# A hybrid attention and S5 layer: GpSimd's tables in parts of three instructions, the chunk operator in its own frame, parameters behind a longer wait

## The chip, the core and the metric

One core of one Trainium2 chip. The time is the device time of one execution in microseconds; three executions were timed, and one more was profiled. PE is TensorE, PEld its weight loads, DVE VectorE, ACT ScalarE, POOL GpSimd, SP SyncE (here only a DMA queue); ACTq is the DMA issue on ACT's queue.

## The reference, cut to what matters

```python
h = rms_norm(x, norm_gain)                       # (2048, 1024)
q, k, v, z_attn, u_ssm, z_ssm, g = split(h @ w_in)
attn = windowed_gqa(q, k, v, sink, rel_table) * silu(z_attn)
# S5: 32 groups of 16 channels, 64 complex states, two directions
a_bar = exp(lam * dt); b_bar = b * (a_bar - 1) / lam
xs = associative_scan(x_t = a_bar * x_{t-1} + b_bar u_t)     # forwards and backwards
y = d * u + sum over directions of Re(c x)
ssm = glu(gelu(y)) * silu(z_ssm)
merged = sigmoid(g_attn) * (attn @ wa) + sigmoid(g_ssm) * (ssm @ ws)
out = rms_norm(x + merged @ w_out) * final_norm_gain
```

All in float32 of (1, 2048, 1024). The matrix products are made of three float32r products each: a value is split into a high part (a copy to float32r) and a low part (the value less its high part).

## The kernel before, in words

**Order of work.** The program is one hand-written order of instructions; each engine takes its own in that order. The projections run as a main line: a weight of 128 output columns is loaded by SP, its high part `wh` is copied by ACT (L163), its low part `wl` subtracted by POOL in four instructions (L155), and 24 matmuls a token block (`mm3`, L220 to L222, three for each of eight slices) add up into one of three PSUM banks "pj", which ACT or DVE empties (`evac`). `wnext` splits a weight one ahead of the one in use. Side chains are generators. At fixed places of the main line (`turn`: after every sixth matmul of a projection) each side gets half its rate as credit and runs a step, up to its next `yield`, while credit is above zero.

**Stage 1** makes h of block b+1 (`make_h`, a side with RATE1) beside six projections of block b. At block 2 `ssm_params` starts: it issues its DMAs from SP's queue (a, dt, b, c, eye, d), then, from the next projection on as a side with rate RATEP, transposes of a, dt and c on PE (L478, L486), and some 300 short instructions on DVE (L441), six a step. After block 3 `drain(pr)` runs what is left.

**Stage 2** is the other projections for blocks 2 and 3 (rate RATE2), three gate weights for all blocks with h of blocks 0 and 1 read back (`h_split`), then blocks 0 and 1. Beside it runs `chain`: first `ssm`, later attention, later the preparation of the last stage. The last stage (GLU, branches, output) has no part in the change.

**The scan** (`ssm`) goes through 8 chunks of four groups, one `frame` each, 19 steps a frame. A position is one of T = 8 in a piece; a piece is one of M = 256. For a chunk:
- `prep_w` (POOL, 12 instructions of 128x256 in `product`, L692 to L694): the table `wt`; `mats` transposes it on PE (L775, banks "s2") and splits it into Wh, Wl (L778, L769).
- `prep_e` (POOL, 6 instructions for each half of a chunk): tables `ec`, `es` of the phases; `mirror_e` copies their mirrored half (ACT, L724).
- `prep_o` (DVE, 6 instructions of 128x512): the table `wo`; `split_o` splits it into ws.
- `zmat`: the chunk operator. `sign_o` (ACT, L739, L741) negates half of `wo`; matmuls with `wo` (L800) and with c (L807) fill two "s2" banks; copies (L808, L809) and one instruction (L810) on DVE make Z of 128x240, stored to DRAM (L904); `load_m` (four DMAs from ACT's queue) reads it back shifted, and `split_m` splits it into Mh, Ml.
- `inject` (PE L837, ACT L838, L839) makes X; `rotate` (DVE L846 to L849), `scan` (DVE L858), `rotate` back, for each half; `high_h` (ACT L865) and `low_h` (DVE L870) split the result into Hh, Hl; `emit` (PE L880 with M and U, L884 with ws and H, ACT L888) makes y, two steps a half.

Before, `frame(i)` for chunk i had, by step: 1 inject 0 and 2 inject 1 with the end of zmat(i); 3 rotate of half 0, store of Z, inject 2; 4 scan, inject 3; 5 rotate back, load_m, mats(i+1); 6 prep_e(i+1, 0), mats; 7 prep_w(i+2), split_o; 8 split_m, high_h; 9 low_h, rotate of half 1; 10 scan; 11 rotate back, prep_e(i+1, 1); 12 and 13 emit half 0; 14 high_h; 15 low_h, mirror_e(i+1, 0); 16 prep_o(i+1), split_u; 17 and 18 emit half 1, split_u, mirror_e(i+1, 1), load_u(i+2) and sign_o(i+1); 19 the L800 matmuls of zmat(i+1).

Banks: "pj" 3, "s1" 2, "s2" 2. wt, wo, ws, Z, M and H have one buffer each, ec and es two.

Of the kernel before, what the change touches and what calls it, by code (L numbers as in the profile page):

```python
# [7 lines left out]
F32 = mybir.dt.float32  # L8
# [3 lines left out]
AF = mybir.ActivationFunctionType  # L12
# [12 lines left out]
M = S // T  # L25
GB = 4
RATE1 = 1.336
RATEP = 2.2
RATE2 = 1.237
RATE3 = 1.499  # L30
WLAG = 2
# [6 lines left out]
def kernel(  # L38
# [404 lines left out]
    def ssm_params(pool):  # L443
# [224 lines left out]
    def ssm(pool):  # L668
# [7 lines left out]
        def bc(t, i, wide):  # L676
            return t[:, i * GB:(i + 1) * GB].unsqueeze(3 if wide else 2).to_broadcast(sh)

        def product(o, p, q, eng):

            for n, (a, b, c, d, op) in enumerate(
                ((p[0], q[0], p[1], q[1], ALU.subtract), (p[0], q[1], p[1], q[0], ALU.add))
            ):
                for g in range(0, o[n].shape[1], 2 if eng is Q else GB):
                    if eng is Q:
                        gs = slice(g, g + 2)
                        tmp = [pool.tile([128, 2, T, C], F32, tag=f"t{m}", name=f"t{m}") for m in range(2)]
                    else:
                        gs = slice(0, GB)
                        r = rtile().rearrange("p g r m -> p g (r m)")  # L690
                        tmp = [r[:, m].rearrange("p (g j c) -> p g j c", g=GB, c=C) for m in range(2)]
                    eng.tensor_tensor(tmp[0], a[:, gs], b[:, gs], ALU.mult)  # L692
                    eng.tensor_tensor(tmp[1], c[:, gs], d[:, gs], ALU.mult)  # L693
                    eng.tensor_tensor(o[n][:, gs], tmp[0], tmp[1], op)  # L694

        def rtile():
            return pool.tile([128, 2, 2, M], F32, tag="rt", name="rt")
# [128 lines left out]
        def inject(i, g):  # L826

            s = st[i]
            if g % 2 == 0:
                X = pool.tile([128, 2, 2, M], F32, tag="X", name="X", bufs=3)  # L830
                s.setdefault("X", {})[g // 2] = X
                V.memset(X[:, :, :, 0:1], 0.0)
            X = s["X"][g // 2][:, g % 2]
            pt = bank("s1").rearrange("p (r m) -> p r m", r=2)
            for n in range(2):
                for m, (a, b) in enumerate(((0, 0), (0, 1), (1, 0))):
                    PE.matmul(pt[:, n], s["W"][a][:, n, g], s["U"][g // 2][b][:, g % 2], start=m == 0, stop=m == 2)  # L837
            A.activation(X[f, :, 1:M], pt[f, :, 0:M - 1], AF.Copy)  # L838
            A.activation(X[b_, :, 1:M], pt[b_, :, M - 1:0:-1], AF.Copy)  # L839
# [52 lines left out]
        def frame(i, zs):  # L892
# [6 lines left out]
            yield  # L899
            inject(i, 1)  # L900
            next(zs, None)
            yield
            rotate(i, 0, 0)
            A.dma_start(out=zS[i], in_=st[i].pop("z"))  # L904
            inject(i, 2)
            yield
            scan(i, 0)
            inject(i, 3)
            yield
            rotate(i, 0, 1)  # L910
            load_m(i)
            if nx:
                next(ms)
            yield
            if nx:
                prep_e(nx, 0)
                next(ms)
            yield
            if nx:
                next(ms, None)  # L920
            if nn:
                prep_w(nn)
            split_o(i)
            yield
            split_m(i)
            high_h(i, 0)
            yield
            low_h(i)
            rotate(i, 1, 0)
            yield  # L930
            scan(i, 1)
            yield
            rotate(i, 1, 1)
            if nx:
                prep_e(nx, 1)
            yield
            yield from emit(i, 0)
            yield
            high_h(i, 1)
            yield  # L940
            low_h(i)
            if nx:
                mirror_e(nx, 0)
            yield
            if nx:
                prep_o(nx, V)
                split_u(nx, 0)
            yield
            yield from emit(i, 1)
            if nx:  # L950
                split_u(nx, 1)
                mirror_e(nx, 1)
                if nn:
                    load_u(nn, 0)
                    load_u(nn, 1)
                zn = zmat(nx)
                next(zn)
                yield
                next(zn)
                nz.append(zn)  # L960
                yield
            st.pop(i)

        raw_o, ph, nz = {}, {}, []
        load_u(0, 0)
        load_u(0, 1)
        prep_w(0, V)
        prep_e(0, 0)
        prep_e(0, 1)
        yield  # L970
        prep_o(0, V)
        yield
        yield from mats(0)
        split_u(0, 0)
        split_u(0, 1)
        zn = zmat(0)
        next(zn)
        mirror_e(0, 0)
        mirror_e(0, 1)
        yield  # L980
        next(zn)
        nz.append(zn)
        load_u(1, 0)
        load_u(1, 1)
        prep_w(1)
        yield
        for i in range(NB):
            yield from frame(i, nz.pop())


    def bias_vectors(pool):
# [736 lines left out]
```

## Time and profile before

| | |
|---|---|
| median of three executions | 1532.38 us (1530.95 to 1532.45) |
| profiled execution | 1529.46 us, its span 1527.7 us |
| PE busy | 1421.8 us, 93% of the span |
| PEld, DVE, ACT, POOL busy | 76%, 68%, 43%, 42% |
| mean granted clock of PE | 0.975 of full |
| DMA | 121 GB/s over the span |

Stage 1 ends near 180 us of the span, the scan near 690, the second stage near 1087. A busy share is a mean over stages; what a change is worth is read from the stage it is in. A row of the waits names the engine and line that stood still, what ended the wait, and the time in all, the count and the longest. A row of a timeline has the start in us from the start of the span, the duration in us, engine, line, operation, what it writes and reads, the count of merged instructions, and in brackets the idle time before it and what ended it.

### The profile page before, as it was taken

What the parts mean: (1) busy time and instruction counts of PE and PEld (TensorE: products, weight loads), DVE (VectorE), ACT (ScalarE), POOL (GpSimd) and SP (SyncE); (2) the same over time, 40 slices, a digit from 0 to 9 for tenths busy, and PEclk for the clock granted to TensorE, in tenths of its full rate; (3) what the DMA queues carried; (4) which work ended last, traced back from release to release, by engine and by line L of the source; (5) the groups of instructions that cost most, each with busy time, mean ns of one, the idle gap of its engine ahead of it and who ended that gap; (6) DMA issues with size and microseconds to landing.
All of it is one profiled execution on the core that took longest, in us unless ns stands there. A gap on an engine that the chain in (4) does not pass through costs nothing.

```text
span 1527.7 us, 19701 instructions
## 1 busy us (share of the span) xinstructions
PE 1421.8 (93%) x6933; PEld 1155.5 (76%) x6933; DVE 1038.0 (68%) x1970; ACT 655.8 (43%) x1197; POOL 641.2 (42%) x683
## 2 busy tenths in 40 slices
PE   7989898998888989799999999999988998999998
PEld 6767786776777768688877788888766886877886
DVE  3327987878759768566898888874578376376442
ACT  6332153353433424434666666664444143243111
POOL 5520288669659574733111111113267053153320
PEclk9999999999999989999999999999999999999999
DMA  7442232232232322446222333325676376376341
GB/s 263 152 107 74 81 99 71 78 120 76 88 100 64 119 83 87 127 146 168 90 87 90 97 97 97 97 91 149 196 201 188 119 188 182 109 183 187 111 126 69
DMA packets 240722, 185.47 MB, mean 121 GB/s; under 512 B 57920, under 2 KB 202432, under 8 KB 240624
## 3 DMA queue, kind: packets, MB, share of 16 engines
q10 hardware_dynamic: 118192, 107.89, 24.2%
q1 hardware_dynamic: 122432, 76.34, 16.8%
q8 instruction: 54, 0.88, 0.2%
q14 instruction: 44, 0.36, 0.1%
HBM read 126.56 MB, written 57.62 MB: 121 GB/s over the span
## 4 chain that ended last, share of the span: by engine, by line
PE 43%; DVE 14%; POOL 13%; DMA 6%; issue 6%; ACT 5%; ACTq 1%; POOLq 0%; SPq 0%; DVEq 0%
PE pj L220 8%; PE pj L222 8%; PE pj L221 8%; POOL wl L155 3%; PE s L1574 3%; POOL t L692 3%; PE s L1575 3%; PE s L1576 3%; POOL t L693 3%; DMA yt<-yS 3%; PE s L1145 2%; PE s L1092 2%; PE s L1129 2%; POOL wt L694 2%; DVE X L847 1%
## 5 line engine op out<-in xcount | busy, mean ns | idle before, releaser
L155 POOL TENSOR_TENSOR wl<-raw,wh 128x256 fp32r<-128x256 f32 x380 | 348.8, 949 | 598.4 <-ACT wh L163 584.1
L222 PE MATMUL pj<-hh,wl 128*128 128x512 f32 x976 | 389.3, 399 | 33.0 <-POOL wl L155 33.0
L220 PE MATMUL pj<-hh,wh 128*128 128x512 f32 x976 | 395.8, 406 | 0.0
L221 PE MATMUL pj<-hl,wh 128*128 128x512 f32 x976 | 388.1, 398 | 0.0
L222 PEld LDWEIGHTS pj<-hh,wl 128*128 128x128 f32 x976 | 187.7, 192 | 77.1 <-POOL wl L155 35.6
L220 PEld LDWEIGHTS pj<-hh,wh 128*128 128x128 f32 x976 | 187.6, 192 | 36.8 <-issue 3.1
L221 PEld LDWEIGHTS pj<-hl,wh 128*128 128x128 f32 x976 | 187.6, 192 | 34.8
L163 ACT ACTIVATE wh<-raw 128x1024 fp32r<-128x1024 f32 x96 | 100.7, 1051 | 17.8 <-DMA raw<-in_w_branch_ssm_dram 4.4
L1574 PE MATMUL s<-woh,mh 128*128 128x512 f32 x256 | 102.4, 400 | 5.0 <-DVE xr L1581 5.0
L1575 PE MATMUL s<-wol,mh 128*128 128x512 f32 x256 | 101.9, 398 | 0.0
L1576 PE MATMUL s<-woh,ml 128*128 128x512 f32 x256 | 101.8, 398 | 0.0
L1109 ACT ACTIVATE p<-p,sml 128x384 f32<-128x384 f32 (+1 forms) x128 | 75.8, 595 | 16.8 <-DVE sml L1105 16.8
L1618 POOL TENSOR_TENSOR sm<-sm,mhalf 128x1 f32<-128x1 f32 x15 | 8.3, 552 | 169.9 <-DVE sm L1617 133.3
L1132 ACT ACTIVATE ph<-s 128x512 fp32r<-128x512 f32 x92 | 54.3, 590 | 58.1 <-PE s L1129 58.1
L404 ACT ACTIVATE st<-pj,bg 128x512 f32<-128x512 f32 x64 | 44.0, 687 | 77.0 <-PE pj L222 74.8
L1093 DVE CUSTOM_DVE_ANT_0 p<-s,bias 128x384 f32<-128x384 f32 (+1 forms) x128 | 68.4, 534 | 12.6 <-PE s L1092 12.1
L1134 DVE TENSOR_TENSOR pl<-s,ph 128x512 fp32r<-128x512 f32 x92 | 63.3, 688 | 18.3 <-ACT ph L1132 16.9
L1581 DVE TENSOR_TENSOR xr<-xr,s 128x512 f32<-128x512 f32 x32 | 21.9, 685 | 69.2 <-PE s L1576 69.2
L849 DVE TENSOR_TENSOR X<-X,rt 128x510 f32<-128x510 f32 x64 | 62.4, 1015 | 1.1
L1574 PEld LDWEIGHTS s<-woh,mh 128*128 128x128 f32 x256 | 48.4, 189 | 18.8 <-DVE xr L1581 7.2
L1092 PE MATMUL s<-kst,qs 128*128 128x384 f32 (+1 forms) x256 | 61.7, 342 | 0.6 <-issue 0.6
L1614 ACT ACTIVATE jk<-xr 128x1024 bf16<-128x1024 f32 x15 | 15.9, 1057 | 97.7 <-DVE xr L1581 97.7
(307 smaller groups left out, 3054.1 us busy)
## 6 DMA issues: line engine op xcount, KB each, us to landing
raw<-in_w_in_dram SPq DMA_DIRECT2D x59, 512.0 KB
gS<-st ACTq DMA_DIRECT2D x64, 256.0 KB
gt<-gS ACTq DMA_DIRECT2D x64, 256.0 KB
x<-in_x_dram SPq DMA_DIRECT2D x16, 512.0 KB
raw<-in_w_branch_attn_dram SPq DMA_DIRECT2D x32, 256.0 KB
raw<-in_w_branch_ssm_dram SPq DMA_DIRECT2D x32, 256.0 KB
out_dram<-xr ACTq DMA_DIRECT2D x15, 512.0 KB
xr<-in_x_dram SPq DMA_DIRECT2D x12, 512.0 KB
```

The lines of the kernel that those rows point to most:

```text
L155: eng.tensor_tensor(lo[:, ks], r[:, ks], hi[:, ks].bitcast(F32), ALU.subtract)
L163: A.activation(res[0], r, AF.Copy)
L220: PE.matmul(pt, w[0][:, k], r[0][:, k], start=start and k == 0, stop=False)
L221: PE.matmul(pt, w[0][:, k], r[1][:, k], start=False, stop=False)
L222: PE.matmul(pt, w[1][:, k], r[0][:, k], start=False, stop=stop and k == kt - 1)
L1092: PE.matmul(pt[:, 0:w], s["qs"][:, h], kst[:, r, kv, k0 * 128:k1 * 128], start=r == 0, stop=r == 1)
L1093: V.tensor_tensor_reduce(out=p[:, h, 0:w], in0=pt[:, 0:w], in1=bias[:, kv * 4 + h, r0:r1:-1], scale=1.0, scalar=0.0, op0=ALU.add, op1=ALU. ...
L1109: A.activation(p[:, h, 0:w], p[:, h, 0:w], AF.Exp, bias=nm[:, j:j + 1], accum_out=den[:, j:j + 1])
L1134: return lambda: V.tensor_tensor(pl, pt, ph.bitcast(F32), ALU.subtract)
L1574: PE.matmul(pt, mh[k][:, ts_], wo[0, n][:, k], start=k == 0, stop=False)
L1575: PE.matmul(pt, mh[k][:, ts_], wo[1, n][:, k], start=False, stop=False)
L1576: PE.matmul(pt, ml[k][:, ts_], wo[0, n][:, k], start=False, stop=k == KD - 1)
```

## The change

Four edits. (1) `product` on POOL no longer issues its instructions at once: it puts parts of three (two products and their sum or difference, for two groups) on a list `work`, and `slot()`, which takes the place of each `yield` of the frame but those inside `emit`, issues the first of the list if its count is even or more than three parts wait. `drain_work` issues all, once, ahead of chunk 0. (2) zmat(i) runs in frame i and no longer at the end of frame i-1: its sign_o at step 2, its L800 matmuls at steps 3 and 4, the rest at step 5; the store of Z is at step 6, load_m at 8, split_m at 10. mirror_e(i, 1) moves to step 4 of frame i, prep_e(i+1, 0) to step 5, prep_w(i+2) to step 8; an empty step is put in ahead of emit, so that what follows is one step later. A frame still has 19 steps; the whole scan has 157 in place of 156. (3) Z's two copies from PSUM go from DVE to ACT. (4) After its loads `ssm_params` yields nine times in place of once, and RATEP goes from 2.2 to 2.6.

```diff
-RATEP = 2.2
+RATEP = 2.6
...
-        yield 0.5
+        for _ in range(9):
+            yield
...
+        work = []
         def product(o, p, q, eng):
+            def part(n, a, b, c, d, op, gs):
...
+                eng.tensor_tensor(tmp[0], a[:, gs], b[:, gs], ALU.mult)
+                eng.tensor_tensor(tmp[1], c[:, gs], d[:, gs], ALU.mult)
+                eng.tensor_tensor(o[n][:, gs], tmp[0], tmp[1], op)
...
                     if eng is Q:
+                        work.append(lambda n=n, x_=x_, g=g: part(n, *x_, slice(g, g + w)))
                     else:
+                        part(n, *x_, slice(g, g + w))
...
+        def slot():
+            count[0] += 1
+            if work and (count[0] % 2 == 0 or len(work) > 3):
+                work.pop(0)()
+            yield
...
-            V.tensor_copy(Z[:, 0:112], pb[:, 0:112])
-            V.tensor_copy(Z[:, 112:240], pf[:, 0:128])
+            A.activation(Z[:, 0:112], pb[:, 0:112], AF.Copy)
+            A.activation(Z[:, 112:240], pf[:, 0:128], AF.Copy)
...
+        def frame(i):
...
+            zs = zmat(i)
             inject(i, 0)
+            yield from slot()
             next(zs)
             inject(i, 1)
+            yield from slot()
+            rotate(i, 0, 0)
+            next(zs)
+            inject(i, 2)
+            yield from slot()
+            scan(i, 0)
+            next(zs)
+            inject(i, 3)
+            if i > 0:
+                mirror_e(i, 1)
+            yield from slot()
             next(zs, None)
+            rotate(i, 0, 1)
+            if nx:
+                prep_e(nx, 0)
+            yield from slot()
             A.dma_start(out=zS[i], in_=st[i].pop("z"))
             if nx:
                 next(ms)
+            yield from slot()
             if nx:
                 next(ms)
+            split_o(i)
+            yield from slot()
+            load_m(i)
+            high_h(i, 0)
             if nx:
                 next(ms, None)
             if nn:
                 prep_w(nn)
+            yield from slot()
             low_h(i)
             rotate(i, 1, 0)
+            yield from slot()
+            split_m(i)
             scan(i, 1)
+            yield from slot()
             rotate(i, 1, 1)
             if nx:
                 prep_e(nx, 1)
+            yield from slot()
+            yield from slot()
             yield from emit(i, 0)
...
```

## Rows read from the trace of the kernel before

**Rows 1.** Waits of PE, 187 to 690 us, and one ahead of them (total, times, longest).
```profile
PE pj L222 <- POOL wl L155: 33.0, 6, 7.4
PE s L800 <- ACT wo L739: 16.8, 7, 8.1
...
PE s L486 <- DMA sm<-in_ssm_c_re_dram: 8.1, 1, 8.1
```

**Rows 2.** Windows from first rotation to first rotation: length, busy PE, PEld, DVE, ACT, POOL, clock.
```profile
272.50:329.20 56.70, 51.88 (x288) 42.38 (x287) 47.81 (x54) 23.46 (x38) 40.26 (x38) 0.97 0.28 90
...
sum 433.00, PE 383.18 PEld 314.80 DVE 328.26 ACT 175.51 POOL 311.83; mean PE 54.74 PEld 44.97 DVE 46.89 ACT 25.07 POOL 44.55
```

**Rows 3.** Windows of 8 us behind waits of PE; the clock stands behind POOL's busy time.
```profile
245.90:253.90 8.00, 8.00 (x31) 6.58 (x32) 7.39 (x7) 4.89 (x8) 7.84 (x7) 0.76 0.43 131
...
486.60:494.60 8.00, 7.99 (x24) 6.35 (x25) 6.78 (x6) 2.17 (x3) 7.84 (x7) 0.65 0.22 66
549.10:557.10 8.00, 7.94 (x28) 6.40 (x29) 7.32 (x7) 3.28 (x6) 7.84 (x8) 0.79 0.42 131
568.10:576.10 8.00, 7.92 (x45) 6.02 (x46) 0.28 (x1) 2.81 (x6) 2.79 (x4) 0.63 0.48 147
631.70:639.70 8.00, 7.95 (x51) 6.23 (x52) 0.28 (x1) 3.91 (x7) 5.79 (x9) 0.76 0.52 161
```

**Rows 4.** Timeline of POOL: first of 18 table instructions, and the weight behind them.
```profile
222.84 1.07 POOL L692 TENSOR_TENSOR t<-eh_re,el_re 128x256 f32<-128x256 f32 x1
...
244.68 5.21 POOL L155 TENSOR_TENSOR wl<-raw,wh 128x256 fp32r<-128x256 f32 x4
```

**Rows 5.** POOL's groups of lines, 187 to 690 us (busy, mean ns, idle before); one of its waits.
```profile
L155 POOL TENSOR_TENSOR wl<-raw,wh 128x256 fp32r<-128x256 f32 x114 | 119.9, 1082 | 120.4 <-ACT wh L163 120.4
L692 POOL TENSOR_TENSOR t<-wi_re,bx_im 128x256 f32<-128x256 f32 x14 | 15.6, 1111 | 1.1
...
POOL ec L694 <- DVE X L847: 15.1, 4, 5.1
```

**Rows 6.** Waits of ACT, 187 to 690 us.
```profile
ACT hh L1245 <- DMA raw<-hS: 14.7, 4, 9.8
ACT Wh L778 <- DMA Ml<-zS: 11.6, 6, 3.1
```

**Rows 7.** Timelines of DVE and PE in chunks 3 and 6.
```profile
391.46 1.22 DVE L846 TENSOR_TENSOR rt<-X,es 128x1020 f32<-128x1020 f32 x1 [0.45 <-ACT X L839]
...
430.44 2.90 DVE L870 TENSOR_TENSOR Hl<-X,Hh 64x1024 fp32r<-64x1024 f32 x2 [3.73 <-ACT Hh L865]
...
436.88 0.28 PE L880 MATMUL s<-U1h,Mh 128*128 128x256 f32 x1
...
454.77 1.22 DVE L846 TENSOR_TENSOR rt<-X,es 128x1020 f32<-128x1020 f32 x1 [0.45 <-ACT X L839]
...
579.08 1.22 DVE L846 TENSOR_TENSOR rt<-X,es 128x1020 f32<-128x1020 f32 x1 [0.45 <-ACT X L839]
...
612.96 2.90 DVE L870 TENSOR_TENSOR Hl<-X,Hh 64x1024 fp32r<-64x1024 f32 x2 [1.13 <-ACT Hh L865]
```

**Rows 8.** Timeline of DVE: four scans, twice.
```profile
334.85 2.42 DVE L858 TENSOR_TENSOR_SCAN X<-rho,X 128x255 f32<-128x255 f32 x4
...
355.00 4.11 DVE L858 TENSOR_TENSOR_SCAN X<-rho,X 128x255 f32<-128x255 f32 x4
```

**Rows 9.** Timelines of DVE and PE around the parameters.
```profile
114.82 0.19 DVE L480 COPY sm<-s 128x32 f32<-128x32 f32 x1
...
125.11 0.75 DVE L277 SCALAR_TENSOR_TENSOR hl<-s,ngain,hh 128x512 fp32r<-128x512 f32 x1 [6.05 <-ACT hh L276]
...
186.95 0.69 DVE L692 TENSOR_TENSOR rt<-wi_re,bx_re 128x512 f32<-128x512 f32 x1
...
117.14 2.15 PE L486 MATMUL s<-ident,sm 128*128 128x128 f32 x8 [8.11 <-DMA sm<-in_ssm_c_re_dram]
...
189.80 1.09 PE L775 MATMUL s<-ident,wt 128*128 128x128 f32 x4 [4.02 <-issue]
```

More of the change, by code (lines that the diff above doesn't have):

```diff
@@ L677, in bc, with drain_work @@
             return t[:, i * GB:(i + 1) * GB].unsqueeze(3 if wide else 2).to_broadcast(sh)
+        work = []
         def product(o, p, q, eng):
[L681 to L684, printed above, removed]
+            def part(n, a, b, c, d, op, gs):
+                if eng is Q:
+                    tmp = [pool.tile([128, 2, T, C], F32, tag=f"t{m}", name=f"t{m}") for m in range(2)]
+                else:
+                    r = rtile().rearrange("p g r m -> p g (r m)")
+                    tmp = [r[:, m].rearrange("p (g j c) -> p g j c", g=GB, c=C) for m in range(2)]
+                eng.tensor_tensor(tmp[0], a[:, gs], b[:, gs], ALU.mult)
+                eng.tensor_tensor(tmp[1], c[:, gs], d[:, gs], ALU.mult)
+                eng.tensor_tensor(o[n][:, gs], tmp[0], tmp[1], op)
+            for n, x_ in enumerate(((p[0], q[0], p[1], q[1], ALU.subtract), (p[0], q[1], p[1], q[0], ALU.add))):
+                w = 2 if eng is Q else GB
+                for g in range(0, o[n].shape[1], w):
                     if eng is Q:
-                        gs = slice(g, g + 2)
-                        tmp = [pool.tile([128, 2, T, C], F32, tag=f"t{m}", name=f"t{m}") for m in range(2)]
-                    else:
[L689 to L694, printed above, removed]
+                        work.append(lambda n=n, x_=x_, g=g: part(n, *x_, slice(g, g + w)))
+                    else:
+                        part(n, *x_, slice(g, g + w))
+        def drain_work():
+            while work:
+                work.pop(0)()
+        count = [0]
+        def slot():
+            count[0] += 1
+            if work and (count[0] % 2 == 0 or len(work) > 3):
+                work.pop(0)()
+            yield
         def rtile():
@@ L890, in emit @@
                 store(chan(yS, i * GB + half * 2 + j), Y[:, j * M:(j + 1) * M])
-        def frame(i, zs):
+        def frame(i):
             nx = i + 1 if i + 1 < NB else None
@@ L896, in frame @@
             ms = mats(nx) if nx else None
+            zs = zmat(i)
             inject(i, 0)
+            yield from slot()
             next(zs)
-            yield
             inject(i, 1)
+            yield from slot()
[9 more added lines that the diff above has]
+            yield from slot()
             next(zs, None)
-            yield
-            rotate(i, 0, 0)
+            rotate(i, 0, 1)
+            if nx:
+                prep_e(nx, 0)
+            yield from slot()
             A.dma_start(out=zS[i], in_=st[i].pop("z"))
[L905 to L911, printed above, removed]
             if nx:
                 next(ms)
-            yield
+            yield from slot()
             if nx:
-                prep_e(nx, 0)
                 next(ms)
-            yield
+            split_o(i)
+            yield from slot()
+            load_m(i)
+            high_h(i, 0)
             if nx:
@@ L935, in frame @@
                 prep_e(nx, 1)
-            yield
+            yield from slot()
+            yield from slot()
             yield from emit(i, 0)
-            yield
+            yield from slot()
             high_h(i, 1)
-            yield
+            yield from slot()
             low_h(i)
@@ L943, in frame @@
                 mirror_e(nx, 0)
-            yield
+            yield from slot()
             if nx:
@@ L947, in frame @@
                 split_u(nx, 0)
-            yield
+            yield from slot()
             yield from emit(i, 1)
@@ L951, in frame @@
                 split_u(nx, 1)
[L952 to L961, printed above, removed]
+            if nn:
+                load_u(nn, 0)
+                load_u(nn, 1)
             st.pop(i)
-        raw_o, ph, nz = {}, {}, []
+            yield from slot()
+        raw_o, ph = {}, {}
         load_u(0, 0)
@@ L969, in ssm @@
         prep_e(0, 1)
+        drain_work()
         yield
@@ L975, in ssm @@
         split_u(0, 1)
-        zn = zmat(0)
-        next(zn)
         mirror_e(0, 0)
         mirror_e(0, 1)
-        yield
-        next(zn)
-        nz.append(zn)
         load_u(1, 0)
@@ L987, in ssm @@
         for i in range(NB):
-            yield from frame(i, nz.pop())
+            yield from frame(i)
     def bias_vectors(pool):
```

7 lines of the change are left out of this document (removed).

## The prediction

> **What bounds the kernel now.** The page says TensorE (PE) is busy for 93% of the span, so time is won where PE stands still. I read the waits of PE first, for the stretch in which the SSM (the scan branch) runs beside the projections [rows 1]: 33.0 us in six waits for `wl`, the low part of a projection weight, which GpSimd (POOL) computes; 16.8 us in seven waits of the chunk operator's first matmuls (L800) for the negated `wo`, which ScalarE (ACT) writes after VectorE (DVE) has made it; and, ahead of that stretch, 8.1 us before the parameters' transposes (L486). Then the windows by chunk (one chunk is four groups; a frame is one chunk's 19 steps): seven chunks, from one first rotation to the next, take 433.0 us, in which PE is busy for 383.2 [rows 2].
>
> A wait costs more than its length. In the 8 us after each longer wait PE is busy, but its granted clock is 0.63 to 0.79 of full, that is, part of the stretch at 1.2 GHz in place of 2.4 [rows 3]. The loss is 8 x (1 - clock): for the six waits for `wl` 1.9, 1.7, 2.1, 1.9, 2.8 and 1.7, together 12.1 us (first, fifth and last shown), for the last two waits at L800 3.0 and 1.9, together 4.9.
>
> Why `wl` is late stands in POOL's timeline [rows 4]: from 222.84 us on, 18 table instructions (prep_e, then prep_w) run in a row, and the four pieces of `wl` behind them start at 244.68, 21.8 us later.
>
> **The change, part by part.**
>
> *Tables in parts.* No instruction is removed: 24 table instructions a chunk, about 1.1 us each, and `wl` at 4 x 1.08 = 4.3 us a weight [rows 5]. They now go out three at a time (3.3 us), one part at a step whose count is even, or at any step with more than three parts waiting. A chunk without waits takes (433.0 - 33.0 - 12.1 - 16.8 - 4.9) / 7 = 52.3 us, 2.75 a step; a step comes each 1.6 turns and a weight lasts 8 turns, so a weight lasts 5 steps, 13.6 us. POOL needs 4.3 us of that for `wl`, and has 2 to 3 parts (7 to 10 us) beside it: it fits, where before up to 12 + 6 instructions could stand ahead. I walked the counter through the frames: in chunks 2 and 4 the parts leave at five steps in a row (8 to 12), 16.5 us in 13.8, so a `wl` emitted right behind them comes some 2.5 us late; in chunks 1, 3 and 5 there are gaps. Taken: 45.1 us come back (33.0 + 12.1), less 5. Bounds: all 45.1, or nothing. A part of prep_e can itself wait for the rotation that reads its buffer, up to 5.1 us as before; what queues behind it on POOL is `wl`, whose 5 us of slack cover that.
>
> *The chunk operator in its own frame.* Its first matmuls move from the third step after prep_o to the fifth (frame step 3), so DVE's six table instructions and ACT's negation have 5.5 us more: 16.8 + 4.9 us come back. The longest, 8.1 us, is another thing: ACT stands there behind splits of `h` that wait for loads, 14.7 us in four [rows 6]; ACT still runs these in order ahead of X and of U, so I leave 4 us of it. Bounds: 0 and 10.
>
> Behind the moved pieces: Z's two small copies go from DVE to ACT, which is busy for under half of the span; but both "s2" banks now wait for them one step before mats(nx) takes them, where it was three. One step is 2.75 us, so I take 1 us in all; bounds 0 and 7 x 2.75 = 19. The store of Z (ACT's queue) goes from step 3 to 6 and waits for DVE's L810, now behind a scan; load_m's four DMAs go from 5 to 8 and wait for that store, as now (11.6 us in six [rows 6]). Behind them on ACT stand the evacuations of the projections; three "pj" banks, two projections of 6 us, cover that. If that cover is gone PE waits the same 2 us a chunk. Ml has two steps to land in place of three, and emit comes a step later: nothing. SP's queue gets nothing new in the frame. mirror_e(i,1) moves to step 4 (rival below). One step is added to the chain in all, 1.6 turns: it ends beside projections, nothing.
>
> *What is late next: DVE.* In chunk 3, from the first rotation (391.46) to the end of the last Hl (430.44 + 2.90) DVE works for 41.9 us nearly without a gap, and emit's second half, which needs Hl, starts on PE only 3.5 us later (436.88) [rows 7]. Over the seven chunks that stretch is 36.8 (chunk 6, the last, also shown) to 41.9, mean 39.6. From there to the next first rotation are 17.9 us here, 1.6 of them the wait at L800; the mean without waits is 15.5, and one step with the operator's matmuls (2.9) leaves this leg: 12.6. So DVE's round is 52.2 us on average against PE's 52.3: both bind. Taking the longer of the two chunk by chunk gives 6 us more than PE's alone; I take 7. Bounds: 0, or 20 if POOL, now beside DVE all the time, stretches it by 2 us a chunk more, as the four scans of half a chunk took 2.42 us with POOL mostly idle and 4.11 beside its tables [rows 8].
>
> *Parameters.* The transposes go from the side's first turn to its seventh (1.3 steps a turn: 2, 3, 4, 6, 7, 8, 10). The 8.1 us wait goes: the loads were there at 117.1 [rows 9], and six turns of six matmuls at 0.23 us, two groups of make_h's transposes (1.2) and a new wait of about 2 us for scaled `x` (DVE until 114.9) bring PE to 120.3. But PE isn't the end of this path. DVE is busy with the parameters from 114.82 to 186.95, with one gap of 6.05 us, and only then makes the first table, for which PE waits 4.0 us at 189.80 [rows 9]. Now DVE starts at 120.3; work of 72.1 - 6.3 us less the two hl it has done before (1.3) ends at 184.8. So 2 us of 8.9 (8.1 and 0.8 of clock) are gained, and PE's wait ahead of 189.80 grows to some 10 us. Bounds: 8.9 gained, or 4 lost if the 6 us gap comes again.
>
> **Sum.** 66.8 - (5 + 4 + 1 + 7) + 2 = 51.8 us less than the profiled execution's 1529.46: 1477.7. The median of the runs shown is 2.9 us above that execution, so about 1481.
>
> **Rivals.**
> - *All of it comes.* DVE keeps clear and parameters too: 1532.4 - 66.8 - 8.9 = 1457. Against it: DVE's 39.6 us without a gap [rows 7]. Chance 0.13.
> - *`wl` stays late.* POOL knows no steps: it runs its queue in order, and parts that leave at steps 8 to 12 are still one block. Then the 21.7 us of L800 and the 2 come: 1509. For it: five steps in a row in two chunks; against: `wl` now gets in between. Chance 0.12.
> - *DVE and POOL get in each other's way.* In chunk 1, the shortest, DVE is busy 47.8 and POOL 40.3 of 56.7 us, so at least 31 us at once [rows 2]. If such overlap is one waiting for the other, a chunk can't get under 56.7: 7 x 56.7 = 397 in place of 433, and 2: 1494. (The Trainium skill, "SBUF — State Buffer", section "SBUF: two separate sides", speaks for this rival: the two engines share a port pair that one instruction locks for its whole length while the other blocks. The scans' 4.11 against 2.42 us agree in direction, but they don't double, so I don't take it whole.) Chance 0.13.
> - *Slower.* mirror_e(i,1) stands in ACT's queue at step 4, ahead of Z's copies and after X's evacuation, and needs the last part of prep_e, which now leaves at step 17 or 19, or in chunk 0 one step into the next frame. If POOL is more than 11 us (four steps) behind there, ACT stops, and PE with it at mats. Two parts and a `wl`, 10.9 us, and 2 of clock, in seven chunks are 90 us, against 66.8 + 2 won: 1554. It decides at a backlog of 11 us; against it, POOL waits 120 us in this stage for `wh` [rows 5]. Chance 0.07.
>
> **Chances and range.** Forecast 0.55. 0.2% (3 us) is about what a measurement of this kernel can tell from no change. All cases but the last are faster: 0.92; the last nearly always slower: 0.06; between: 0.02. The forecast's own range, with its bounds mixed, is 1465 to 1500; to hold 8 in 10 the range goes down near the full gain and up to late `wl`: 1461 to 1511.
>
> **What would show it.** In the waits of PE: `wl` from 33.0 us to under 8, L800 from 16.8 to under 4, L486 gone, the wait at L775 ahead of the first frame about 10, and new waits for Hl (L884) of some 7. Chunks of 52 to 55 us from first rotation to first rotation, granted clock 0.97 or more in them. On POOL, `wl` between parts of three. I am wrong if PE stands at mats or L800 in each frame, if chunks stay at 57 or more, or if the first table comes as early as PE does.

## The result, and the profile after

1508.45 us, the median of four executions (1507.22 to 1511.3), against 1532.41 us of the kernel before beside it: ratio 0.9854, interval 0.9842 to 0.9866. That is 24 us less, where 51.8 were forecast; the time lies near the upper end of the stated range (1461 to 1511). The profiled span is 1506.4 us (before 1527.7).

The page's busy times and chain of the kernel after, and below them the chain of the kernel before:

```profile
PE 1418.1 (94%) x6933; PEld 1154.6 (77%) x6933; DVE 1041.8 (69%) x1954; ACT 659.9 (44%) x1213; POOL 637.9 (42%) x683
...
PE 39%; DVE 26%; issue 7%; DMA 6%; ACT 5%; POOL 4%; ACTq 1%; DVEq 0%; POOLq 0%; SPq 0%
...
PE 43%; DVE 14%; POOL 13%; DMA 6%; issue 6%; ACT 5%; ACTq 1%; POOLq 0%; SPq 0%; DVEq 0%
```

On the chain (the work that ended last, followed back) DVE now has 26% (14% before) and POOL 4% (13%). The waits of PE from 183 to 690 us of the kernel after, which answer to [rows 1]:

```profile
PE s L901 <- DVE Ml L749: 11.7, 6, 4.0
PE s L796 <- issue: 11.7, 1, 11.7
PE s L858 <- DVE U0l L749: 7.0, 6, 1.6
PE s L796 <- POOL wt L694: 5.5, 1, 5.5
PE s L821 <- ACT wo L760: 4.0, 1, 4.0
PE s L905 <- DVE Hl L891: 3.7, 2, 3.5
```

(Lines moved: mats L775 is L796, zmat L800 is L821, inject L837 is L858, emit L880 and L884 are L901 and L905, rotate L846 is L867, Hl L870 is L891.) The 33.0 us for `wl` are gone wholly, and of 16.8 us for `wo` one wait of 4.0 is left. In their place stand waits for low parts that DVE makes: Ml, U0l, Hl, 22.4 us. The chunks, from first rotation to first rotation, in the windows of the kernel after (columns as in [rows 2]):

```profile
208.22:271.90 63.68, 56.08 (x317) 45.84 (x308) 47.38 (x46) 24.28 (x39) 48.96 (x51) 0.95 0.28 87
271.90:335.49 63.59, 56.06 (x300) 46.30 (x299) 49.40 (x53) 24.18 (x41) 40.91 (x38) 0.92 0.27 87
335.49:391.38 55.89, 52.39 (x279) 43.19 (x279) 49.77 (x50) 24.39 (x40) 44.25 (x40) 0.97 0.30 94
...
503.77:558.04 54.27, 52.08 (x290) 42.68 (x293) 45.55 (x45) 24.82 (x41) 44.42 (x40) 1.00 0.32 103
558.04:618.30 60.26, 54.37 (x322) 44.59 (x315) 42.47 (x45) 29.18 (x45) 41.55 (x43) 0.98 0.36 109
sum 410.08, PE 379.14 PEld 311.14 DVE 325.50 ACT 178.21 POOL 305.98; mean PE 54.16 PEld 44.45 DVE 46.50 ACT 25.46 POOL 43.71
```

Seven chunks take 410.1 us (433.0 before, [rows 2]). Four of them, chunks 2 to 5, are at 54.3 to 56.5, some 3 us above the forecast of 52.2; chunks 0, 1 and 6 are 5 to 8 us longer than these four's mean of 55.6. The 8 us behind the longer waits, in windows of the kernel after (the clock is the number after POOL's count):

```profile
301.17:309.17 8.00, 8.00 (x36) 6.89 (x37) 7.90 (x7) 0.00 (x0) 7.85 (x7) 0.79 0.23 68
362.70:370.70 8.00, 7.98 (x36) 6.84 (x37) 7.90 (x7) 0.97 (x2) 7.61 (x8) 0.79 0.06 25
420.30:428.30 8.00, 7.95 (x36) 6.71 (x37) 7.90 (x7) 0.60 (x1) 7.76 (x8) 0.79 0.30 94
319.83:327.83 8.00, 8.00 (x30) 7.03 (x31) 7.90 (x9) 1.72 (x3) 5.92 (x6) 0.63 0.27 79
225.58:233.58 8.00, 8.00 (x27) 6.50 (x28) 2.34 (x3) 2.28 (x5) 6.57 (x9) 0.71 0.22 61
616.91:624.91 8.00, 8.00 (x49) 6.04 (x50) 6.54 (x9) 4.40 (x9) 3.28 (x4) 0.63 0.77 217
```

With 8 x (1 - clock), as the prediction reckons it, the first three (Ml) cost 5.0 us more, the next (Hl) 3.0, wt 2.3, L821 3.0. So the waits cost Ml 16.7, U 7.0, Hl 6.7, wt 7.8 and L821 7.0, together 45.2 us, where `wl` and L800 had cost 66.8. The difference, 21.6, less 1.1 us by which PE's first table is later (190.88 in place of 189.80), is 20.5; the spans differ by 21.3. Nothing large is missing from this account.

How Ml and Hl come late shows in the timelines of DVE and PE, chunk 1, kernel after:

```profile
291.39 3.31 DVE L891 TENSOR_TENSOR Hl<-X,Hh 64x1024 fp32r<-64x1024 f32 x2
294.73 1.53 DVE L867 TENSOR_TENSOR rt<-X,es 128x1020 f32<-128x1020 f32 x1
...
299.91 1.20 DVE L749 TENSOR_TENSOR Ml<-Ml,Mh 128x512 fp32r<-128x512 f32 x1
301.03 4.41 DVE L879 TENSOR_TENSOR_SCAN X<-rho,X 128x255 f32<-128x255 f32 x4
...
316.84 2.94 DVE L891 TENSOR_TENSOR Hl<-X,Hh 64x1024 fp32r<-64x1024 f32 x2
...
301.17 0.38 PE L901 MATMUL s<-U0h,Ml 128*128 128x256 f32 x1 [4.04 <-DVE Ml L749]
...
319.83 0.58 PE L905 MATMUL s<-Hl,ws0h 128*128 128x256 f32 x1 [3.49 <-DVE Hl L891]
```

split_m, two steps later than before, now stands behind the rotation of half 1, and emit starts while DVE is still at it.

Ml's load was not late: ACT had made its high part by 292.6 us, and DVE took up the low part at 299.91 without standing for it.

And chunk 0, timelines of POOL, PE, ACT and DVE, kernel after:

```profile
218.37 5.21 POOL L155 TENSOR_TENSOR wl<-raw,wh 128x256 fp32r<-128x256 f32 x4 [0.47 <-ACT wh L163]
223.54 0.61 POOL L692 TENSOR_TENSOR t<-wi_re,bx_im 128x256 f32<-128x256 f32 x1
...
224.81 0.72 POOL L694 TENSOR_TENSOR wt<-t,t 128x256 f32<-128x256 f32 x1
...
225.58 0.69 PE L796 MATMUL s<-ident,wt 128*128 128x128 f32 x2 [5.46 <-POOL wt L694]
...
226.31 0.60 ACT L799 ACTIVATE Wh<-s 128x512 fp32r<-128x512 f32 x1 [7.16 <-PE s L796]
...
227.46 0.71 DVE L749 TENSOR_TENSOR ws0l<-wo,ws0h 128x512 fp32r<-128x512 f32 x1 [3.86 <-ACT ws0h L748]
```

The last part of prep_w(1) went out behind a `wl`; PE, ACT and DVE stood one behind the other for it.

**DVE's round**, means of seven chunks in us, worked out from DVE's timeline. The leg runs from the first rotation to the end of the last Hl, the rest from there to the next first rotation. Idle is the sum of the bracketed waits in the leg; what is left beside busy and idle are small gaps between instructions.

```
                         leg    busy  idle    rest   chunk
before                   39.6   37.2   1.9    22.3   61.9
forecast                 39.6                 12.6   52.2
after                    43.5   37.6   5.5    15.1   58.6
after, chunk 0           48.1   37.8   9.8    15.6   63.7
after, chunk 1           47.9   40.4   7.1    15.7   63.6
experiment 2, chunk 0    41.4   38.5   2.5    16.1   57.5
experiment 9             39.4   37.6   1.3    19.1   58.5
```

The forecast's 12.6 counts from the start of emit's second half on PE, which was taken to follow the leg at once. In the kernel before that start lay 0.6 us ahead of the leg's end to 7.7 us behind it. In the kernel after it lies within 0.8 us of the end in six chunks, and in chunk 1 PE stands in emit until the leg has ended (319.83 above), so there the columns compare.

DVE works as long as before; it stands longer in its own leg. In seven chunks it stands 38.7 us there (13.4 before): 16.1 for Hh from ACT (8.8), 8.8 for Z (none), 8.6 for a gate's tanh (3.2), 5.3 for ws (1.3). This is the part that the forecast lacked.

Leg and rest make up the chunk by their definition, so their sum does not show that DVE is full. It is not. First rotations of DVE, kernel after:

```profile
447.87 1.22 DVE L867 TENSOR_TENSOR rt<-X,es 128x1020 f32<-128x1020 f32 x1 [4.63 <-issue]
...
503.77 1.22 DVE L867 TENSOR_TENSOR rt<-X,es 128x1020 f32<-128x1020 f32 x1 [5.92 <-issue]
...
618.30 1.30 DVE L867 TENSOR_TENSOR rt<-X,es 128x1020 f32<-128x1020 f32 x1 [8.90 <-POOL hl L1267]
```

Ahead of each of the seven DVE stands 2.0 to 8.9 us, 32.1 in all, where before it stood 0.5 at most ([rows 7] has three). DVE is late with the low parts in its leg, and has time to spare between the legs.

### The profile page after: what moved, and what is told of

It is laid out like the page before. It is cut to its first block, busy times and chain, and to the rows that moved or that the text cites. A ratio compares the mean times of both kernels' runs of the same rounds, so it can differ in the third digit from the quotient of the medians.

```text
span 1506.4 us, 19697 instructions
## 1 busy us (share of the span) xinstructions
PE 1418.1 (94%) x6933; PEld 1154.6 (77%) x6933; DVE 1041.8 (69%) x1954; ACT 659.9 (44%) x1213; POOL 637.9 (42%) x683
## 4 chain that ended last, share of the span: by engine, by line
PE 39%; DVE 26%; issue 7%; DMA 6%; ACT 5%; POOL 4%; ACTq 1%; DVEq 0%; POOLq 0%; SPq 0%
PE pj L220 7%; PE pj L222 7%; PE pj L221 7%; PE s L1592 3%; PE s L1593 3%; PE s L1594 3%; DVE Hl L891 2%; DMA yt<-yS 2%; DVE X L879 2%; PE s L1163 2%; DVE X L868 2%; PE s L1110 2%; DVE rt L867 2%; DVE X L870 2%; PE s L1147 2%
## 5 line engine op out<-in xcount | busy, mean ns | idle before, releaser
L155 POOL TENSOR_TENSOR wl<-raw,wh 128x256 fp32r<-128x256 f32 x380 | 355.0, 964 | 573.5 <-ACT wh L163 483.7
L220 PE MATMUL pj<-hh,wh 128*128 128x512 f32 x976 | 391.2, 401 | 0.0
L1127 ACT ACTIVATE p<-p,sml 128x384 f32<-128x384 f32 (+1 forms) x128 | 75.8, 594 | 16.3 <-DVE sml L1123 16.1
L867 DVE TENSOR_TENSOR rt<-X,es 128x1020 f32<-128x1020 f32 x32 | 43.3, 1353 | 38.1 <-issue 14.4
L1110 PE MATMUL s<-kst,qs 128*128 128x384 f32 (+1 forms) x256 | 65.7, 339 | 0.0
L1592 PEld LDWEIGHTS s<-woh,mh 128*128 128x128 f32 x256 | 48.5, 189 | 20.5 <-DVE xr L1599 8.9
L870 DVE TENSOR_TENSOR X<-X,rt 128x510 f32<-128x510 f32 x64 | 62.0, 1009 | 1.1
L891 DVE TENSOR_TENSOR Hl<-X,Hh 64x1024 fp32r<-64x1024 f32 x32 | 46.7, 1460 | 17.9 <-ACT Hh L886 17.4
```

The costliest lines, as they stand in the source:

```text
L155: eng.tensor_tensor(lo[:, ks], r[:, ks], hi[:, ks].bitcast(F32), ALU.subtract)
L220: PE.matmul(pt, w[0][:, k], r[0][:, k], start=start and k == 0, stop=False)
L870: V.tensor_tensor(X[:, :, r], X[:, :, r], t[:, :, r], ALU.add if r == back else ALU.subtract)
L891: V.tensor_tensor(H[1][rows], xv, H[0][rows].bitcast(F32), ALU.subtract)
L1110: PE.matmul(pt[:, 0:w], s["qs"][:, h], kst[:, r, kv, k0 * 128:k1 * 128], start=r == 0, stop=r == 1)
L1127: A.activation(p[:, h, 0:w], p[:, h, 0:w], AF.Exp, bias=nm[:, j:j + 1], accum_out=den[:, j:j + 1])
```

## The experiments

Each ratio is to the kernel before, run beside it (medians 1530.4 to 1531.6 us).

**1. split_m a step earlier.**

```diff
             low_h(i)
+            split_m(i)
             rotate(i, 1, 0)
             yield from slot()
-            split_m(i)
             scan(i, 1)
```

> The changed kernel with split_m moved two lines up: in frame step 9, behind low_h and ahead of rotate(i, 1, 0), where it stood in step 10 behind that rotation. Theory A (the order in DVE's queue): PE's wait at L901 for Ml (11.7 us in six, and some 5 us of half clock behind three of them) is only there because Ml's low part stands behind the rotation's four instructions of 5.2 us; it goes, and the time falls from 1508 by 10 to 16 us, to 1492 to 1498. Theory B (DVE's whole round binds): the same wait comes back a few us later at L905 for Hl, and the time falls by 0 to 4 us, to 1504 or more.

1507.59 us, ratio 0.9855 (0.984 to 0.987): nothing gained, theory B. Waits of PE, 183 to 690 us, in this kernel:

```profile
PE s L858 <- DVE U0l L749: 10.6, 8, 2.1
PE pj L220 <- DVE st L401: 5.9, 2, 5.6
PE s L905 <- DVE Hl L891: 5.7, 6, 2.0
```

The 11.7 us for Ml are gone; U0l has 3.6 us more, Hl 2.0, and a "pj" bank that DVE empties is new. These three are DVE's, 22.2 us together where Ml, U0l and Hl had 22.4: the wait moved along its queue, though not to Hl alone as theory B had it.

**2. All tables out behind prep_w(1).**

```diff
         prep_w(1)
+        drain_work()
         yield
         for i in range(NB):
```

> The changed kernel with the four parts of prep_w(1) issued at once ahead of the first frame, as the kernel before did, and all else in parts. Theory A: the wait at L796 for wt in chunk 0 (5.5 us and 2.3 us of clock) goes, and no wait for wl takes its place, since the kernel before had none behind this block: 1508 less 6 to 9, 1499 to 1502. Theory B: twelve instructions in a row make a weight late in chunk 0 again, PE waits at L222 for wl: 1506 to 1510.

1502.64 us, ratio 0.9813 (0.9799 to 0.9827): 5.8 us less than the change: theory A, at its edge (6 to 9 less). The wait for wt is gone and none for `wl` takes its place; chunk 0 takes 57.5 us in place of 63.7, and DVE's idle time in its leg falls from 9.8 to 2.5. The other chunks stay within 1.2 us.

**3. Parameters as before.**

```diff
-RATEP = 2.6
+RATEP = 2.2
...
-        for _ in range(9):
-            yield
+        yield 0.5
```

> The changed kernel with the parameters' edit undone (one yield after the loads, RATEP 2.2). Theory A (DVE's parameter work sets when the first table is there, PE only waits in another place): PE's 8 us at L486 come back, its 11.7 us at L796 shrink to some 4, and the time stays within 3 us of 1508. Theory B (the wait for the loads was a loss of its own): 8 to 10 us slower, 1516 to 1518.

1507.63 us, ratio 0.9846 (0.9833 to 0.986): theory A. The 8 us at L486 are back, and the wait ahead of the first table falls from 11.7 to 4.0: edit (4) only moved the wait.

**4. Lumps again, in the new places.**

```diff
             count[0] += 1
-            if work and (count[0] % 2 == 0 or len(work) > 3):
-                work.pop(0)()
+            drain_work()
```

> The changed kernel with slot() issuing all that waits on the list, so that the tables leave in blocks of 6 and 12 again, in the new frame. Theory A (the parts took away the waits for wl): PE's waits at L222 for wl come back, 25 to 35 us, and 8 to 12 us of clock: 1540 to 1555. Theory B (the new places of prep_e and prep_w in the frame did it, not the parts): under 10 us of waits for wl, 1508 to 1520.

1516.33 us, ratio 0.9909 (0.9895 to 0.9922): the time of theory B, with somewhat more waits for `wl` than it allowed (10 us). Only some of those waits return, in its waits of PE:

```profile
PE pj L222 <- POOL wl L155: 12.8, 3, 4.9
PE s L900 <- DVE Ml L748: 12.1, 6, 4.1
```

With prep_e and prep_w in three different steps, a lump is 6 or 12 instructions and no longer 18 [rows 4]. In the new places the parts are worth 8 us net: the lumps also shorten the wait for wt (2.1 us in place of 5.5) and those for U0l and Hl (4.7 in place of 10.7).

**5. Z's copies back on DVE.**

```diff
-            A.activation(Z[:, 0:112], pb[:, 0:112], AF.Copy)
-            A.activation(Z[:, 112:240], pf[:, 0:128], AF.Copy)
+            V.tensor_copy(Z[:, 0:112], pb[:, 0:112])
+            V.tensor_copy(Z[:, 112:240], pf[:, 0:128])
```

> The kernel after with Z's two small copies back on DVE. Theory A (ACT's queue holds up DVE's round: in the kernel after DVE stands 10.8 us in five waits at L831 for ACT's Z): these waits go, and Ml, U0l and Hl come earlier by part of them; 3 to 8 us under the kernel after, so 1500 to 1505 us. Theory B (DVE is short of time, not held up; two copies more of some 0.3 us are a small load, and ACT's place is taken by another wait): no difference beyond 3 us, 1506 to 1511 us. Rival against both: X's evacuation on ACT is what is late, so that DVE only stands at another line; then DVE's wait moves from L831 to Hl or X, of the same length.

1509.34 us, ratio 0.9863 (0.9848 to 0.9877): nothing. Theory A fell: DVE no longer stands for ACT's Z, and PE's waits stay.

**6. Less work for DVE.** On top of experiment 1, without the four scans of each chunk's second half, so that half of the states are not computed:

```diff
             yield from slot()
-            scan(i, 1)
             yield from slot()
```

> e1_splitm with the four scan instructions of the second half of each chunk left out (so the second half of the scan's states isn't computed): DVE loses some 4.2 us of work a chunk and nothing else changes. Theory A (DVE's round is the bound that stays once Ml's place is mended): the waits at U0l, Hl and the 'pj' bank that stand on DVE (22 us in e1_splitm) fall under 6 us, and the time to some 1490 us (1483 to 1497). Theory B (PE's round, or ACT, binds as well): the waits shift to ACT's and POOL's tiles and the time stays above 1500 us.

1490.02 us, ratio 0.9737 (0.9722 to 0.9751): 17.6 us less than experiment 1, theory A. DVE's busy time falls by 28.9 us over the eight chunks (1039.4 to 1010.5). Its waits of PE for DVE:

```profile
PE s L905 <- DVE Hl L891: 3.6, 1, 3.6
...
PE s L858 <- DVE U0l L749: 1.0, 1, 1.0
...
PE pj L220 <- DVE st L401: 0.9, 1, 0.9
```

22 us of such waits became 5.5. So these waits hang on what DVE does in its leg, and some 60% of what is taken from it comes off the time. The rest doesn't: the wait at L821 grows from 4.9 to 7.5 us, that for `wl` from 1.2 to 2.5, and DVE stands longer ahead of the first rotations (40.1 us in seven, 32.2 in experiment 1).

**7. What helped, together.** Experiments 1, 2 and 5, both U splits ahead of prep_o, and the parameters' transposes divided:

```diff
+                split_u(nx, 0)
+                split_u(nx, 1)
                 prep_o(nx, V)
-                split_u(nx, 0)
...
-        for _ in range(9):
-            yield
+        yield 0.5
...
         for n, op in enumerate(V.ops):
             op()
+            if n == 59:
+                for i, dst in enumerate((cc_re, cc_im)):
+                    ...
```

> The kernel after with five moves: split_m a step earlier (as in e1_splitm), all tables drained behind prep_w(1) in the prologue (as in e2_w1), Z's copies on DVE, U's two low parts both split ahead of prep_o, and the parameters' transposes of a and dt at once with those of c only behind DVE's 60th operation. Theory A (each removes the wait it stands behind): the wait for wt (5.5 and 2.3 of clock), the wait at the first L796 (11.7, back to some 4 to 6) and U's 7.0 go and nothing new comes: some 1490 us (1484 to 1496). Theory B (DVE's round is full, so waits taken away at one tile come back at another): only e2_w1's 6 us and the parameters' 4 to 6, so 1497 to 1503 us.

1489.27 us, ratio 0.9736 (0.9716 to 0.9755): the time of theory A, 41 us under the kernel before beside it. PE's first table starts at 181.5 us (190.9 in the change). The waits for wt and Ml are gone and U0l has 1.9 us; against theory A, L821 has 9.6 in place of 4.0, and 5.2 at a "pj" bank are new. Experiments 2 and 12 give 5.8 and 9.9 of the 19.2 us by themselves, experiments 1 and 5 nothing; the order of U's splits was not run alone.

**8. The parts alone, in the kernel before.** product, slot and drain_work as in the change; every call stays in its place, with

```diff
+                drain_work()
                 mirror_e(nx, 1)
```

> The kernel before with GpSimd's tables in parts alone: same places of prep_e, prep_w, prep_o, zmat, Z, mirror_e and parameters as before. Theory A (the parts are what takes the 33.0 us of waits for wl away): 30 to 45 us less than before, so 1487 to 1502 us, the waits at L800 as before (16.8). Theory B (as e4_lump suggests, where giving the parts up cost 8 us: the new places of the calls did most of it, and the parts little): 8 to 15 us less than before, 1517 to 1524 us, with 15 us or more of waits for wl left. Rival to both: without the new places the last parts of prep_e reach mirror_e late, and PE stands at mats: same as before or slower.

1548.35 us, ratio 1.0119 (1.0102 to 1.0136): slower, as the rival had it, though PE stands at the operator's matmuls and not at mats. Waits of PE:

```profile
PE s L820 <- ACT wo L759: 45.9, 7, 9.6
PE s L904 <- DVE Hl L890: 11.3, 6, 3.8
```

No wait for `wl` is left, as theory A said; but the waits for `wo` went from 16.8 to 45.9. ACT's timeline in this kernel tells why:

```profile
326.17 0.41 ACT L744 ACTIVATE ec<-ec 128x254 f32<-128x254 f32 x1
328.88 0.41 ACT L744 ACTIVATE es<-es 128x254 f32<-128x254 f32 x1 [2.31 <-POOL es L693]
328.89 1.27 ACTq L772 DMA_DIRECT2D U0l<-uS  x2
330.21 1.19 ACTq L772 DMA_DIRECT2D U1l<-uS  x2
331.44 0.63 ACT L759 ACTIVATE wo<-wo 128x512 f32<-128x512 f32 x1 [2.15 <-DMA U0l<-uS]
```

The mirroring waits for the last part, made later now; behind it on ACT's queue stand the issues of four loads of U, and then the negation of `wo`. That this is what costs is tested next.

**9. The same with the mirroring out of the way.**

```diff
-                drain_work()
-                mirror_e(nx, 1)
...
                 nz.append(zn)
+                drain_work()
+                mirror_e(nx, 1)
```

> e8_parts with the mirroring of the second rotation table (mirror_e(nx,1), and the flush of GpSimd's list ahead of it) moved behind the operator's first matmuls, nothing else. Theory A (in e8_parts ACT stands at the mirroring for GpSimd's last part, 23.6 us in seven, and the negation of wo, ahead of which PE stands 45.9 us at L820, is behind it in ACT's queue): the waits at L820 fall to 10 to 20 us, wl stays at nothing, and the time falls by 25 to 45 us, to 1503 to 1523 us. Theory B (wo is late because DVE makes it late, one step ahead of its use, and the waits for wl had only hidden that): the waits at L820 stay above 35 us and the time above 1535 us.

1507.19 us, ratio 0.9847 (0.9831 to 0.9863): theory A. 41 us come from the place of the mirroring and of the `drain_work` ahead of it. `wl` costs nothing, `wo` 11.4 us in six; Hl has 10.3, its high part 8.9. This is the time of the whole change, without moving the operator, with Z's copies on DVE and the parameters as before. DVE's idle time in the leg is 1.3 us a chunk here, less than in the kernel before, though the waits for `wl` are gone.

**10 and 11. No negation on ACT; then half of prep_o on POOL.** On top of experiment 7:

```diff
-                eng.tensor_tensor(o[n][:, gs], tmp[0], tmp[1], op)
+                if neg and n == 1:
+                    eng.scalar_tensor_tensor(o[n][:, gs], tmp[0], -1.0, tmp[1], ALU.mult, ALU.subtract)
```

> e7_best with the negation of wo folded into DVE's last table instruction (and the small negated cc made on DVE), so that ACT has no part ahead of the operator's first matmuls. Theory A (the 9.6 us at L821 in e7_best are ACT's queue, in which the negation stands behind splits of h that wait for their loads): these waits go and the time is 1478 to 1484 us. Theory B (DVE has no room: what ACT's negation hid is DVE being late): the wait stays at L821 with DVE's wo as releaser or moves to Hl and U0l, and the time is 1486 to 1492 us.

1488.86 us, ratio 0.9725 (0.9707 to 0.9743): the wait at L821 falls from 9.6 us to 1.0 and the time stays; theory B.

```diff
+                e = Q if neg == 2 and n == 0 else eng
```

> e10_neg with half of prep_o (three of DVE's six table instructions a chunk, 3.3 us) given to GpSimd in two parts of three. Theory A (DVE's round still binds, as leaving out 4.2 us of scans a chunk showed): another 7 to 15 us come, 1465 to 1478 us. Theory B (by now PE's own round binds): the same as e10_neg within 3 us. Rival: GpSimd, which has 6.5 us more to do a chunk, is late with wo, wt or wl: new waits of over 10 us for its tiles and a time above e10_neg's by 5 us or more.

1536.65 us, ratio 1.0035 (1.0019 to 1.0052), 48 us above experiment 10: the rival. In its waits of PE:

```profile
PE s L820 <- POOL wo L697: 39.6, 9, 9.1
```

**12. The parameters' transposes divided, alone** (the last two hunks of experiment 7).

> The kernel after with only the parameters' transposes changed: those of a and dt at once, as before the change, those of c only behind DVE's 60th operation on the parameters. Theory A (DVE's work on the parameters sets the first table, and it starts 5 us late in the kernel after because its inputs wait for the side's seventh turn): the first matmul at L796 starts 8 to 10 us earlier than 190.9, PE's wait there falls from 11.7 to some 5 us, and the time by 5 to 9 us, to 1499 to 1504 us. Theory B (what comes early is given back in the following chunks, since DVE's round is full): the first table comes early and the time stays at 1506 to 1510 us.

1498.55 us, ratio 0.9795 (0.9777 to 0.9813): 9.9 us less than the change, theory A and slightly more. PE's first table starts at 183.1 us in place of 190.9 and PE waits 5.1 there; the seven chunks take 408.2 us (410.1), so nothing of it is given back. DVE begins the parameters at 114.88 us and is done at 180.22 (121.95 and 188.03 in the change).

**13 and 14. The gates' evacuation off DVE**, in the change and in experiment 7:

```diff
-            V.scalar_tensor_tensor(st, th, 1.0, pt, ALU.add, ALU.mult)
-            store((zaS if kind == "za" else zsS)[row, tok], st)
+            A.activation(st, pt, AF.Copy)
+            A.activation(th, th, AF.Copy, bias=1.0)
+            Q.tensor_tensor(st, th, st, ALU.mult)
+            stores.append((3, (zaS if kind == "za" else zsS)[row, tok], st))
```

> The kernel after with the gates' evacuation (16 projections of za and zs) taken off DVE: ACT copies the bank to st and adds 1 to th, GpSimd multiplies the two, and the store goes out two ticks later. In the kernel after, chunk 1 takes 63.6 us where chunks 2 to 5 take 55.6: DVE's queue holds these evacuations behind rotations and a scan (294.73 to 310.59), ACT stands 17.28 us behind them, and Hh and Hl are late. Theory A (this is what chunk 1 loses, 8 us, with its clock): chunk 1 at 56 to 58 us, the others as before, 1499 to 1504 us. Theory B (chunk 1 is long because DVE has too much to do in it, and the evacuations, 0.7 us each, are a small part): chunk 1 above 61 us, 1505 to 1510 us. Rival: GpSimd, with 2 us more for each such projection, makes wl late again: new waits for wl and no gain or a loss.

1511.84 us, ratio 0.9888 (0.9872 to 0.9904). Neither theory, since theory A wanted 56 to 58 us for chunk 1. Chunk 1 falls from 63.6 to 58.8 us and its leg from 47.9 to 42.5, so the evacuations in DVE's queue were 4.8 of the 8 us by which it was longer than chunks 2 to 5; but chunk 2 rises from 55.9 to 60.5, since POOL is late with `wl` (5.8 us in two waits): the rival.

> e7_best with the same evacuation. Theory A: chunk 1 from 61.4 to 55 to 57 us and the 5.2 us wait for the 'pj' bank gone, 1479 to 1485 us. Theory B: chunk 1 stays above 60 us, 1486 to 1492 us.

1493.51 us, ratio 0.9765 (0.9752 to 0.9778): 4 us worse than experiment 7, with 9.2 us of waits for `wl`. Neither theory; the rival of 13 again: chunk 1 takes 59.4 us (61.4 in experiment 7), chunk 2 64.6 (54.4).

**15. The mirroring alone moved, in the kernel before.**

```diff
-                mirror_e(nx, 1)
...
                 nz.append(zn)
+                mirror_e(nx, 1)
```

> The kernel before with mirror_e(nx,1) alone moved behind the operator's first matmuls; the tables go out in lumps of six and twelve as before. Theory A (e9_mirror's 23 us are the parts' work, and the mirroring cost nothing where the tables were made early): waits for wl stay near 33 us, those at L800 near 17, and the time within 4 us of the kernel before, 1526 to 1534 us. Theory B (ACT's place of the mirroring was part of the L800 waits all along): the waits at L800 fall under 8 us and the time by 8 us or more, under 1523 us.

1530.37 us, ratio 0.9994 (0.9981 to 1.0007), with `wl` at 32.8 us and L800 at 15.7: theory A. Moving the mirroring gains nothing by itself, and the parts by themselves lose 18 us (experiment 8): the 23 us of experiment 9 need both.

## Why the prediction was wrong

- **Tables in parts: right, and the forecast low by 5.** "45.1 us come back (33.0 + 12.1), less 5": all 45.1 did. That five parts in a row make a `wl` late showed in no wait. Experiments 9 and 15 show that in the old places the parts do it, once the mirroring is out of their way; in the new places lumps would have cost only 8 us (experiment 4).
- **The chunk operator: near.** 21.7 less 4 was forecast; L821 kept 4.0 us and 3.0 of clock, behind `h` as named. Z's copies and the "s2" banks cost PE nothing (forecast 1; experiment 5), though DVE stands 8.8 us in its legs for them.
- **split_m, failed.** The step is "Ml has two steps to land in place of three, and emit comes a step later: nothing". The load was in time; the low part wasn't, since it queues on DVE behind a rotation. 16.7 us, where I asked about the transfer and not about the queue. Yet mending it alone brought nothing (experiment 1): it belongs with the next point.
- **DVE's round, the step that failed.** "So DVE's round is 52.2 us on average against PE's 52.3: both bind ... I take 7." That DVE is late next was right, its size was not: Ml, U and Hl cost 30.4 us against 7. The leg was carried over from the kernel before as 39.6 and came out at 43.5, with the same work (37.2 and 37.6) and 5.5 us of idle time in place of 1.9. The rest was put at 12.6 and came out at 15.1, and in 4.6 of these DVE itself stands ahead of the next first rotation. So the picture of a DVE that works without a gap, and whose round is the sum of its work, failed too: in the kernel after DVE is busy for 46.5 of 58.6 us. What binds is its lateness inside the leg; experiment 6 shows that PE's waits for its low parts hang on that.
- **Why the leg grew** is known in part. In chunk 0 it is the wait for wt (experiment 2: 48.1 to 41.4 us, and 5.8 us off the time). In chunk 1 it is in part the gates' evacuations, which went to POOL only at the price of a late `wl` (experiment 13). Elsewhere DVE stands for Hh and Z from ACT; Z's copies back on DVE gained nothing (experiment 5, where 34.7 of the 38.7 us stay), and the cause stays open. That the waits for `wl` had given the other engines time to catch up isn't borne out: in experiment 9 those waits are gone, and with the order of before the leg stays at 39.4 with 1.3 us of idle time. With the parameters as before in the new order (experiment 3) the idle time is 5.8 us a chunk. So it came with the new order of the frame.
- **The bound of 20** rested on POOL beside DVE all the time. In the legs POOL was busy for 32.7 us a chunk before and 32.4 after, so there was no more overlap there than before.
- **wt in chunk 0, not costed.** I drained the list ahead of chunk 0 in my walk and missed that prep_w(1), emitted behind it, now leaves in parts through the first frame. 5.5 us and 2.3 of clock; experiment 2 gives 5.8 back.
- **Parameters: the mechanism right, 3 us off.** The wait at L486 goes, one of 11.7 us comes (forecast "some 10"); the first table is 1.1 us later where I had 2 gained. DVE began at 121.95 us (forecast 120.3) and was done at 188.03 (forecast 184.8). Experiment 12, where it begins 7.1 us earlier, has the first table 7.8 earlier. Experiment 3 begins as early (115.00) and is done only at 187.59: with PE's wait for the loads, a gap of 6.5 us in DVE's work is back.
- **The sum.** +5 (`wl`), -3 (L821), +1, -23 (DVE's round against 7), -8 (wt) and -3 make some 31 us less than the forecast of 51.8, that is about 21; the spans differ by 21.3.
- **The signs.** That "chunks stay at 57 or more" was named as a sign of being wrong, and it holds for the mean of 58.6 and for three of the seven; the new wait was looked for at Hl (3.7 us) and came mostly at Ml and U0l (18.7).
- **The rivals.** "`wl` stays late" gave 1509, the time that came, for a reason that was wrong. "DVE and POOL in each other's way" held that no chunk gets under 56.7 us; four did. In the chunk of 54.27 us DVE is busy 45.55 and POOL 44.42, so 35.7 at least at once. The Trainium skill, "SBUF — State Buffer", section "SBUF: two separate sides", says that an instruction of one of the two engines can hold the shared port pair for its whole length while the other blocks. The 35.7 us do not contradict that, since busy times may hold waiting for the pair, which no run here separates; they show only that it did not hold a chunk at 56.7. The slower rival's mechanism was real, as experiments 8 and 9 show at another place of the mirroring; in the change PE's only wait at mats is that for wt.

## What to carry to other kernels

A stretch of another engine's timeline that was measured in the old order, its idle time included, is not the stretch of the new order: here a leg of 39.6 us became 43.5 with the same work, and stayed 39.4 where the order was kept. So ask of each moved piece what stands ahead of it on the queue of the engine that makes it last, and whether that engine will itself stand for someone. Check too that the engine is full before its round is called a bound: DVE was late with its low parts and idle ahead of the next chunk. A lump cut into parts ended later here than the lump: look for who waits for its last part, and what stands behind that waiter in order (moving that one place was worth 41 us, from 1548 to 1507). When waits of one engine's tiles follow each other in its order, mending one can move the time to the next (experiment 1); what helped here was less work on that engine (experiment 6) or an earlier start (9.9 us for the parameters).

## What the runs showed of the hardware

An instruction of POOL of 128x256 took 0.61 to 0.72 us while DVE stood (223.54 and 224.81 us in chunk 0 above) and about 1.1 us as a mean over the scan [rows 5]. DVE's four scans took 2.42 us with POOL mostly idle and 4.11 beside its tables [rows 8], and 4.41 at 301.03 in the kernel after, where POOL is busy for 7.85 of the 8 us that follow. So both engines' instructions are longer where the other is busy. The change did not add to it in DVE's legs: POOL was busy there for 32.7 us a chunk before and 32.4 after, DVE for 37.2 and 37.6.
